# Second attention of a two-layer trunk: reciprocal per head, place of the short rows' parts, banks of the logits, and order of the projections

## The chip, the cores and the metric

The kernel runs on one core of a Trainium2 chip. The metric is the device time of one execution in microseconds (us); the kernel before took 1237.31 us in the median of three runs (1236.33 to 1238.17).

The engines are called as the profile calls them: PE is TensorE (matmuls; PEld its weight loads), DVE is VectorE, ACT is ScalarE, POOL is GpSimd, SP is the queue that issues DMAs. Each engine works through its own instructions in the order of the program and waits where an operand is not there or a buffer is not free.

## The reference, cut to what matters

512 positions of width 1024 go through two layers and a final norm. Layer 0 is a mixer of block-sparse and windowed attention and an MLP; layer 1 is the "forgetting" attention that the change touches, and a second MLP. Cut to that attention:

```python
def fox_mixer(h, w_in, b_forget, w_out):          # 16 heads of 64, Q = 128
    q, k, v, fz = _split(h @ w_in, ODD_SPLITS)
    ...
    log_f = jax.nn.log_sigmoid((fz + b_forget).astype(jnp.float32))
    cum = jnp.cumsum(log_f, axis=1).transpose(0, 2, 1)
    def block(c):                                 # one block of 128 query rows
        ...
        s = (jnp.einsum('bhqd,bhkd->bhqk', qc, k).astype(jnp.float32) * scale
             + cq[..., None] - cum[:, :, None, :])
        p = masked_softmax(s, key_pos[None, :] <= t[:, None])
        return jnp.einsum('bhqk,bhkd->bhqd', p, v).astype(jnp.float32)
    o = lax.map(block, jnp.arange(S // Q))
    ...
    return o.astype(h.dtype) @ w_out
```

## The kernel before, in words

All matmuls that need float32 accuracy are made of parts: an operand is split into a rounded high part and a low part (the rest), and three products are added up in one bank (`mm3`, L129 to L131). `split` makes the parts of a weight: ACT copies the high part (L91), then DVE or POOL subtracts it from the raw weight (L94); the letters of `FOX_LOW` say, tile by tile in the order of use, which of the two.

The stages follow each other: first mixer (0 to about 310 us of the span), first MLP, second attention (`fox`, about 640 to 893 us), second MLP. A scheduler orders every engine's instructions when the program is built; it starts from the order in which the code is written, which in `fox` is the string `FOX_ORDER`: `v0` to `v3` project values of four heads each, `f` makes the forget gates, `k0` to `k7` project queries and keys of a pair of heads (24 matmuls of 512 columns each for q and for k), `p0` to `p7` do the softmax of a pair, and `o01` and the like multiply the outputs of two pairs with the output weights and add them to the residual rows (8 groups of 6 matmuls, each followed by an addition on DVE, L530).

For one head `softmax_t` works on four blocks of query rows, `qi` 3 to 0. Block `qi` sees 128*(qi+1) keys, so a row has 512, 384, 256 or 128 logits; "long rows" are those of qi 3 and 2, "short rows" those of qi 1 and 0. In turn:

- PE makes the logits of a block in two passes into a PSUM bank (L457). The banks come from the tag `s`, which has two; the third block's logits need the bank of the first.
- DVE adds the mask and finds the minimum (L461, written to the tile P), ACT takes the exponential and its sum (L462).
- After two blocks DVE takes their reciprocal (L464) and scales it (L465). This is done twice in a head.
- The long rows' high parts (f16, tile HL) are made by ACT (L473), the short rows' by POOL (L475). The low parts of all rows are made by DVE in one operation with two SBUF inputs (L476).
- When the whole of HL is written, SP issues a transposing DMA to HT (L478).

`turned` widens HT to the parts PTh (ACT, L488) and PTl (POOL, L406); `pv` multiplies them with the values (L499, L500); `combine` (L509, L510) and `split_o` (L406, L515) bring the result into the form that the output projection needs. The list `todo` holds `turned` and `pv` of a head back until the softmax of the next head is written down: the transposition of one head is under way while the next head's logits are worked on. PTh and PTl of a head are ordered behind the instructions that `p_act` and `p_pool` name: the newest exponential of the next head, and its last high part on POOL.

The tiles P, HL, HT, PTh and PTl have two buffers each, and each of the PSUM tags `acc` (projections), `s` (logits), `pt` and `o` has two banks. A projection's bank is freed by its copies and subtractions: for q by ACT L1269 and DVE L402, for k by ACT L1272 and DVE L400, for values by ACT L1220 and DVE L400.

Of the kernel before, what the change touches and what calls it, by code (L numbers as in the profile page):

```python
# [7 lines left out]
F32 = mybir.dt.float32  # L8
# [3 lines left out]
AF = mybir.ActivationFunctionType  # L12
ALU = mybir.AluOpType
AX = mybir.AxisListType

P = 128
S = 512
D = 1024
NT = S // P
# [7 lines left out]
SEG = [0, 128, 384, 768]  # L27
P_UP = 32768.0
PTW = 1280
BANKS = [(0, [(0, 0)]), (512, [(1, 0), (3, 384)]), (1024, [(2, 0)])]  # L30
PTOFF = {0: 0, 1: 512, 3: 896, 2: 1024}
# [11 lines left out]

MIX0_ORDER = "c0 k1 q1 n0 v1 v0 k0 n1 m1 c1 m0 k2 n2 o45 o0 n3 k3 m2 m3 o17 o6 o23"

FOX_ORDER = "v0 f k0 k1 k2 k3 p0 v1 k4 p1 p2 o01 k5 v3 v2 p3 k6 p4 p5 p6 k7 o23 o45 p7 o67"


class Trunk:
# [395 lines left out]
    def softmax_t(self, passes, band):  # L445


        nc = self.nc
        pt = self.pP.tile([P, PTW], F32, tag="P", name=self.nm("P"))
        st = self.sm.tile([P, 3, 4], F32, tag="sst", name=self.nm("sst"))  # L450
        hl = self.pHL.tile([P, 2, PTW], F16, tag="HL", name=self.nm("HL"))
        for q0 in (2, 0):
            for qi in (q0 + 1, q0):
                w = P * (qi + 1)
                ps = self.psum("s")
                for i, (q, k) in enumerate(passes):
                    nc.tensor.matmul(ps[:, :w], q[:, qi * P:(qi + 1) * P], k[:, :w],  # L457
                                     start=i == 0, stop=i == len(passes) - 1)
                seg = pt[:, SEG[qi]:SEG[qi] + w]
                mn, sm = (st[:, a, qi:qi + 1] for a in range(2))  # L460
                nc.vector.tensor_tensor_reduce(seg, ps[:, :w], band[:, S - w:S], 1.0, 3e38, ALU.add, ALU.min, mn)  # L461
                self.p_act = nc.scalar.activation(seg, seg, AF.Exp, bias=mn, scale=-1.0, accum_out=sm)  # L462
            r = st[:, 2, q0:q0 + 2]
            nc.vector.reciprocal(r, st[:, 1, q0:q0 + 2])  # L464
            nc.vector.tensor_scalar(r, r, P_UP, None, op0=ALU.mult)  # L465
            for qi in (q0 + 1, q0):
                r = st[:, 2, qi:qi + 1]
                parts = [(0, min(qi + 1, 3), qi * P)] + ([(3, 4, PTOFF[3])] if qi == 3 else [])
                for j0, j1, off in parts:
                    seg = pt[:, SEG[qi] + j0 * P:SEG[qi] + j1 * P].rearrange("p (j c) -> p j c", c=P)  # L470
                    view = lambda a: hl[:, a, off:].rearrange("p (j c) -> p j c", c=P)[:, 0:3 * (j1 - j0 - 1) + 1:3, :]
                    if q0 == 2:
                        nc.scalar.activation(view(0), seg, AF.Copy, scale=r)  # L473
                    else:
                        self.p_pool = nc.gpsimd.tensor_scalar(view(0), seg, r, 1.0, op0=ALU.mult, op1=ALU.mult)  # L475
                    nc.vector.scalar_tensor_tensor(view(1), seg, r, view(0), op0=ALU.mult, op1=ALU.subtract)  # L476
        t = self.pHT.tile([P, 2 * PTW // P, P], F16, tag="HT", name=self.nm("HT"))
        nc.sync.dma_start_transpose(t, hl.rearrange("p a b -> p (a b)"))  # L478
        return t

    def turned(self, t):


        tv = t.rearrange("p (a b) c -> p a (b c)", a=2)
        hi = self.pPT.tile([P, PTW], FR, tag="PTh", name=self.nm("PTh"))
        lo = self.pPT.tile([P, PTW], FR, tag="PTl", name=self.nm("PTl"))
        with self.tc.issue_after(self.p_act.ins):
            self.nc.scalar.activation(hi, tv[:, 0], AF.Copy)  # L488
        with self.tc.issue_after(self.p_pool.ins):
            self.round(lo, tv[:, 1])  # L490
        return hi, lo

# [689 lines left out]
    def fox(self, hs):  # L1182
        self.phase, self.pieces = FOX_LOW, 0
        nc, I = self.nc, self.I
        w = I["odd_w_in"][0]
        wo = I["odd_w_out"][0]
        lo, hi = slice(0, HD), slice(HD, P)
        with ExitStack() as cx:
# [4 lines left out]
            self.pHT = pool("fHT", 2)  # L1193
            o2 = pool("fo", 2)
            a1 = cx.enter_context(self.tc.tile_pool(name="attf1", bufs=1))
            wv = self.cols(w, [(2048, 2304), (3072, 3088)])
            x = self.norm_t(hs, self.row_tile(I["mix_norm"][1], "g"))
            zt = a1.tile([P, NT, 16], F32, name="zt")
            band = a1.tile([P, S], F32, name="mband")
# [101 lines left out]
            st, o = {}, {}  # L1301

            def step(op, arg):
                if op == "v":
                    values(int(arg))
                elif op == "f":
                    forget()
                elif op == "k":
                    st[int(arg)] = qk(int(arg))
                elif op == "p":  # L1310
                    pair(int(arg), st[int(arg)])
                elif op == "o":
                    pairs = [int(a) for a in arg]
                    if pairs[-1] not in o:
                        behind()
                    self.out_proj(wo, pairs, [o[a] for a in pairs], hs)

            for s in FOX_ORDER.split():
                step(s[0], s[1:])
# [41 lines left out]
```

## Time and profile before

| | |
|---|---|
| median of three runs | 1237.31 us (1236.33 to 1238.17) |
| the profiled execution | 1239.53 us |
| its span, first to last instruction | 1237.8 us |
| mean granted TensorE clock | 0.991 |
| second attention, 640 to 900 us: PE busy | 240.26 of 260 us |
| DVE, ACT and POOL busy there | 193.38, 159.35 and 111.87 us |

All durations are of the one profiled execution. Busy times count an instruction from its start to its end; matmuls follow each other before the one ahead has ended, so the mean of one matmul (383 ns for 512 columns) is longer than the step from one to the next. "PE acc L129 <- DVE Q L402: 2.6, 3, 1.6" reads: PE, at line 129 with a bank `acc`, stood idle 2.6 us in all and three times, 1.6 us at the longest, until DVE had finished line 402. The granted clock (PEclk) is the share of full speed that PE was given in a stretch.

### The profile page before, as it was taken

The numbers are of one execution on the slowest core, as the hardware profiler recorded it, in microseconds if no ns is written. First come the engines' busy times: TensorE is split into PE (matmuls) and PEld (weight loads), VectorE is DVE, ScalarE is ACT, GpSimd is POOL, SyncE is SP. The second block draws the span as 40 slices with busy tenths as digits, with TensorE's granted clock in tenths as the row PEclk, the third lists the DMA queues.
The fourth block names the chain that finished last, engine by engine and source line by source line (L and its number), as shares of the span: only waits on it lengthen the run. The fifth ranks groups of instructions, "written<-read, shape, count | busy, mean of one in ns | idle before, by whom it ended". The sixth has DMA issues, their size and how long they took to land.

```text
span 1237.8 us, 16953 instructions
## 1 busy us (share of the span) xinstructions
PE 1201.4 (97%) x6055; PEld 1011.2 (82%) x6055; DVE 986.7 (80%) x1683; ACT 672.7 (54%) x1211; POOL 481.3 (39%) x470
## 2 busy tenths in 40 slices
PE   9999999999999999999999889998899999999997
PEld 7879987887888888888887777887798888888886
DVE  6877678788878897789775778749787898789875
ACT  6447666675654455445436666647455444544542
POOL 3434457553543233323003453535345323332214
PEclk9999999999999999999999989999999999999999
DMA  7961232131533324333024544644563333332301
GB/s 231 336 179 53 86 102 78 51 112 52 153 102 102 102 87 119 106 99 95 26 69 130 117 100 112 135 123 89 150 169 104 96 92 120 102 103 88 98 1 69
DMA packets 183440, 134.25 MB, mean 108 GB/s; under 512 B 47875, under 2 KB 158635, under 8 KB 183356
## 3 DMA queue, kind: packets, MB, share of 16 engines
q1 hardware_dynamic: 183196, 132.94, 38.3%
q8 instruction: 48, 0.79, 0.3%
q14 instruction: 36, 0.29, 0.1%
q10 hardware_dynamic: 160, 0.23, 0.1%
HBM read 120.27 MB, written 7.64 MB: 103 GB/s over the span
## 4 chain that ended last, share of the span: by engine, by line
PE 61%; DVE 8%; ACT 2%; DMA 2%; issue 2%; POOL 1%; DVEq 0%; ACTq 0%; POOLq 0%
PE s L1123 12%; PE acc L131 11%; PE acc L129 11%; PE acc L130 11%; PE o L1123 6%; PE pt L1123 3%; DVE HL L476 2%; DMA HT<-HL 2%; DVE P L461 1%; DVE whl L94 1%; PE s L131 1%; PE s L130 1%; PE s L129 1%; PE s L457 1%; DVE x L530 1%
## 5 line engine op out<-in xcount | busy, mean ns | idle before, releaser
L129 PE MATMUL acc<-xhi,whl 128*128 128x512 f32 (+1 forms) x768 | 293.9, 383 | 2.8 <-DVE Q L402 2.5
L131 PE MATMUL acc<-xhi,whl 128*128 128x512 f32 (+1 forms) x768 | 294.3, 383 | 1.4 <-POOL whl L94 0.8
L130 PE MATMUL acc<-xlo,whl 128*128 128x512 f32 (+1 forms) x768 | 292.9, 381 | 0.0
L94 DVE TENSOR_TENSOR whl<-raw,whl 128x1024 fp32r<-128x1024 f32 (+2 forms) x110 | 161.7, 1473 | 84.8 <-ACT whl L91 68.5
L1026 POOL TENSOR_TENSOR r<-r,yrow 128x512 f32<-128x512 f32 x64 | 98.3, 1536 | 317.4 <-ACT r L1025 317.4
L91 ACT ACTIVATE whl<-raw 128x1024 fp32r<-128x1024 f32 (+1 forms) x139 | 145.0, 1048 | 47.5 <-PE acc L131 27.9
L131 PEld LDWEIGHTS acc<-xhi,whl 128*128 128x128 f32 x768 | 144.5, 188 | 30.4 <-DVE whl L94 1.6
L129 PEld LDWEIGHTS acc<-xhi,whl 128*128 128x128 f32 x768 | 144.4, 188 | 30.5 <-issue 2.4
L1123 PE MATMUL s<-whl,sp 128*128 128x512 f32 x672 | 167.6, 390 | 0.0
L130 PEld LDWEIGHTS acc<-xlo,whl 128*128 128x128 f32 x768 | 144.7, 188 | 26.4
L1123 PEld LDWEIGHTS s<-whl,sp 128*128 128x128 f32 x672 | 126.2, 188 | 26.6
L1077 ACT ACTIVATE whl<-w 128x1024 fp32r<-128x1024 f32 x98 | 103.6, 1059 | 71.2 <-PE s L1123 43.5
L1078 DVE TENSOR_TENSOR whl<-w,whl 128x1024 fp32r<-128x1024 f32 x98 | 134.9, 1378 | 8.5 <-ACT whl L1077 8.5
L1025 ACT ACTIVATE r<-acc 128x512 f32<-128x512 f32 x62 | 37.1, 598 | 117.0 <-PE acc L131 117.0
L94 POOL TENSOR_TENSOR whl<-raw,whl 128x1024 fp32r<-128x1024 f32 x29 | 71.1, 2454 | 51.2 <-ACT whl L91 49.7
L1123 PE MATMUL o<-whl,sp 128*128 128x512 f32 x336 | 88.8, 391 | 0.0
L1083 DVE TENSOR_TENSOR w<-w,w 128x1024 f32<-128x1024 f32 x56 | 82.0, 1464 | 1.0
L1131 DVE TENSOR_TENSOR x<-s,x 128x512 f32<-128x512 f32 x112 | 74.8, 679 | 3.0 <-PE s L1123 3.0
L1123 PEld LDWEIGHTS o<-whl,sp 128*128 128x128 f32 x336 | 63.3, 188 | 13.6
L400 DVE TENSOR_TENSOR sp<-act,sp 128x512 fp32r<-128x512 f32 x64 | 69.5, 1107 | 0.6 <-ACT sp L1034 0.6
L1028 ACT ACTIVATE act<-r 128x512 f32<-128x512 f32 x64 | 40.5, 633 | 45.8 <-POOL r L1026 45.7
L422 ACT ACTIVATE P<-P,sst 128x128 f32<-128x128 f32 (+1 forms) x96 | 53.3, 557 | 14.4 <-DVE sst L421 12.6
(291 smaller groups left out, 2493.9 us busy)
## 6 DMA issues: line engine op xcount, KB each, us to landing
raw<-in_mlp_w SPq DMA_DIRECT2D x72, 512.0 KB
w<-in_mlp_w SPq DMA_DIRECT2D x56, 512.0 KB
raw<-in_odd_w_in SPq DMA_DIRECT2D x22, 512.0 KB
raw<-in_even_w_in SPq DMA_DIRECT2D x20, 512.0 KB
band<-bias_dram SPq DMA_DIRECT2D x24, 256.0 KB
bias_dram<-bias_rows SPq DMA_DIRECT2D x16, 320.0 KB
raw<-in_even_w_out SPq DMA_DIRECT2D x8, 512.0 KB
raw<-in_odd_w_out SPq DMA_DIRECT2D x8, 512.0 KB
```

The costliest lines, as they stand in the source:

```text
L91: nc.scalar.activation(hl[:, 0, :n], raw[:, :n], AF.Copy)
L94: eng.tensor_tensor(hl[:, 1, :n], raw[:, :n], hl[:, 0, :n].bitcast(F32), op=ALU.subtract)
L129: mm(ps, ahl[0], bhl[0], start=first, stop=False)
L130: mm(ps, ahl[0], bhl[1], start=False, stop=False)
L131: mm(ps, ahl[1], bhl[0], start=False, stop=last)
L400: self.nc.vector.tensor_tensor(out, ps, hi.bitcast(F32), op=ALU.subtract)
L1026: nc.gpsimd.tensor_tensor(r, r, row, op=ALU.mult)
L1077: nc.scalar.activation(t[:, 0], src, AF.Copy)
L1078: nc.vector.tensor_tensor(t[:, 1], src, t[:, 0].bitcast(F32), op=ALU.subtract)
L1083: nc.vector.tensor_tensor(out, a_, b_, op=op)
L1123: mm = lambda l, r, first, last: nc.tensor.matmul(ps, l, r, start=first, stop=last, skip_group_check=True)
L1131: nc.vector.tensor_tensor(hv, ps, hv, op=ALU.add)
```

## The change

It has five parts, all of them in the second attention.

1. The reciprocal and its scaling are done once in a head, behind all four exponentials (new L462, L463), on four elements a row instead of twice on two. The scaling multiplies by a small tile `p_up`, filled once, and no longer by a number.
2. Short rows: POOL multiplies P by the reciprocal in place (new L467, two instructions), ACT copies the high parts (new L471, 256 and 128 columns), and POOL subtracts them for the low parts (new L472). Long rows stay with ACT and DVE (new L478, L479). In a head this takes two operations of DVE away, adds two to ACT, and makes two of POOL four.
3. The logits use the banks of `s` and `pt` in turn, so that a head has four.
4. PTh is ordered behind the last high part of the next head and no longer behind its last exponential; PTl behind its last low part on POOL.
5. `FOX_ORDER`: key, query and value projections stand between the pairs of heads one at a time, and `o45` stands behind the last pair.

```diff
-FOX_ORDER = "v0 f k0 k1 k2 k3 p0 v1 k4 p1 p2 o01 k5 v3 v2 p3 k6 p4 p5 p6 k7 o23 o45 p7 o67"
+FOX_ORDER = "v0 f k0 k1 p0 k2 v1 p1 k3 p2 o01 k4 v2 p3 k5 p4 k6 v3 p5 k7 p6 o23 p7 o45 o67"
...
-        for q0 in (2, 0):
-            for qi in (q0 + 1, q0):
-                w = P * (qi + 1)
-                ps = self.psum("s")
...
-            r = st[:, 2, q0:q0 + 2]
-            nc.vector.reciprocal(r, st[:, 1, q0:q0 + 2])
-            nc.vector.tensor_scalar(r, r, P_UP, None, op0=ALU.mult)
-            for qi in (q0 + 1, q0):
...
-                    if q0 == 2:
-                        nc.scalar.activation(view(0), seg, AF.Copy, scale=r)
-                    else:
-                        self.p_pool = nc.gpsimd.tensor_scalar(view(0), seg, r, 1.0, op0=ALU.mult, op1=ALU.mult)
-                    nc.vector.scalar_tensor_tensor(view(1), seg, r, view(0), op0=ALU.mult, op1=ALU.subtract)
+        for qi in (3, 2, 1, 0):
+            w = P * (qi + 1)
+            ps = self.psum("s" if qi % 2 else "pt")
...
+        nc.vector.reciprocal(st[:, 2], st[:, 1])
+        nc.vector.tensor_tensor(st[:, 2], st[:, 2], self.p_up, op=ALU.mult)
+        blocks = lambda v, off, n, step: v[:, off:].rearrange("p (j c) -> p j c", c=P)[:, 0:step * (n - 1) + 1:step, :]
+        for qi in (1, 0):
+            seg = pt[:, SEG[qi]:SEG[qi] + P * (qi + 1)]
+            nc.gpsimd.tensor_scalar(seg, seg, st[:, 2, qi:qi + 1], 1.0, op0=ALU.mult, op1=ALU.mult)
+        for a, off, n in ((0, 0, 2), (2 * P, PTOFF[1], 1)):
+            seg = pt[:, a:a + n * P]
+            h, l = (hl[:, i, off:off + n * P] for i in range(2))
+            self.p_act = nc.scalar.activation(h, seg, AF.Copy)
+            self.p_low = nc.gpsimd.tensor_tensor(l, seg, h, op=ALU.subtract)
+        for qi in (3, 2):
+            r = st[:, 2, qi:qi + 1]
+            for j0, n, off in ((0, 3, qi * P), (3, 1, PTOFF[3]))[:qi - 1]:
+                seg = blocks(pt, SEG[qi] + j0 * P, n, 1)
+                h, l = (blocks(hl[:, i], off, n, 3) for i in range(2))
+                self.p_act = nc.scalar.activation(h, seg, AF.Copy, scale=r)
+                nc.vector.scalar_tensor_tensor(l, seg, r, h, op0=ALU.mult, op1=ALU.subtract)
...
-        with self.tc.issue_after(self.p_pool.ins):
+        with self.tc.issue_after(self.p_low.ins):
             self.round(lo, tv[:, 1])
...
+            self.p_up = a1.tile([P, NT], F32, name="pup")
+            nc.gpsimd.memset(self.p_up, P_UP)
```

What the scheduler makes of it is seen in the order of the built programs. In the rows below a row is a line of the code, an operation, what it writes and reads, and the size; names carry buffer numbers. Line numbers of the change are those of its own text.

On PE, at the first head of the second attention (s and pt are logits' banks, acc a projection's), before:

```order
L131 MATMUL acc_6543<-xhi_6182,whl_6540 128x512
L457 MATMUL s_6794<-K_971_6516,Q_969_6514 128x512
L457 MATMUL s_6799<-K_971_6516,Q_969_6514 128x384
L457 MATMUL s_6794<-K_972_6517,Q_970_6515 128x512
L457 MATMUL s_6799<-K_972_6517,Q_970_6515 128x384
L129 MATMUL acc_6573<-xhi_6182,whl_6570 128x512
L130 MATMUL acc_6573<-xlo_6183,whl_6570 128x512
```

and with the change:

```order
L131 MATMUL acc_6545<-xhi_6184,whl_6542 128x512
L456 MATMUL s_6628<-K_971_6518,Q_969_6516 128x512
L456 MATMUL pt_6633<-K_971_6518,Q_969_6516 128x384
L456 MATMUL s_6628<-K_972_6519,Q_970_6517 128x512
L456 MATMUL pt_6633<-K_972_6519,Q_970_6517 128x384
L456 MATMUL s_6638<-K_971_6518,Q_969_6516 128x256
L456 MATMUL s_6638<-K_972_6519,Q_970_6517 128x256
L456 MATMUL pt_6643<-K_971_6518,Q_969_6516 128x128
L456 MATMUL pt_6643<-K_972_6519,Q_970_6517 128x128
L129 MATMUL acc_6575<-xhi_6184,whl_6572 128x512
```

The head starts at the same place; its four blocks now stand together, while before the logits of 256 and 128 columns stood 22 matmuls further on.

On ACT, at the second head (P, HL and sst with the middle numbers are its tiles, PTh is the first head's), before:

```order
L462 ACTIVATE P_6830,sst_6831<-P_6830,sst_6831 128x128
L473 ACTIVATE HL_6832<-P_6830,sst_6831 128x3x128
L473 ACTIVATE HL_6832<-P_6830,sst_6831 128x128
L473 ACTIVATE HL_6832<-P_6830,sst_6831 128x3x128
L462 ACTIVATE P_7087,sst_7088<-P_7087,sst_7088 128x512
L488 ACTIVATE PTh_6869<-HT_6828 128x1280
L462 ACTIVATE P_7087,sst_7088<-P_7087,sst_7088 128x384
```

and with the change:

```order
L461 ACTIVATE P_6664,sst_6665<-P_6664,sst_6665 128x128
L1277 ACTIVATE K_989_6614<-acc_6575 64x512
L478 ACTIVATE HL_6666<-P_6664,sst_6665 128x3x128
L478 ACTIVATE HL_6666<-P_6664,sst_6665 128x128
L478 ACTIVATE HL_6666<-P_6664,sst_6665 128x3x128
L491 ACTIVATE PTh_6703<-HT_6662 128x1280
L471 ACTIVATE HL_6666<-P_6664 128x128
L471 ACTIVATE HL_6666<-P_6664 128x256
L1274 ACTIVATE Q_1017_6778<-acc_6723 64x512
```

The second head's two short copies now stand behind the first head's PTh, which waits for a transposition; a copy that frees a projection's bank (L1274) stands behind them.

On POOL, at the first two heads, before:

```order
L475 TENSOR_SCALAR HL_6793<-P_6791,sst_6792 128x2x128
L475 TENSOR_SCALAR HL_6793<-P_6791,sst_6792 128x128
L475 TENSOR_SCALAR HL_6832<-P_6830,sst_6831 128x2x128
L475 TENSOR_SCALAR HL_6832<-P_6830,sst_6831 128x128
L406 TENSOR_SCALAR PTl_6870<-HT_6828 128x1280
```

and with the change:

```order
L467 TENSOR_SCALAR P_6625<-P_6625,sst_6626 128x256
L467 TENSOR_SCALAR P_6625<-P_6625,sst_6626 128x128
L472 TENSOR_TENSOR HL_6627<-P_6625,HL_6627 128x128
L472 TENSOR_TENSOR HL_6627<-P_6625,HL_6627 128x256
L406 TENSOR_SCALAR K_985_6602<-K_985_6602 64x512
L94 TENSOR_TENSOR whl_6806<-raw_6802,whl_6806 128x1024
L467 TENSOR_SCALAR P_6664<-P_6664,sst_6665 128x256
L467 TENSOR_SCALAR P_6664<-P_6664,sst_6665 128x128
L406 TENSOR_SCALAR K_989_6614<-K_989_6614 64x512
L472 TENSOR_TENSOR HL_6666<-P_6664,HL_6666 128x128
L406 TENSOR_SCALAR PTl_6704<-HT_6662 128x1280
L472 TENSOR_TENSOR HL_6666<-P_6664,HL_6666 128x256
```

Two instructions of a head became four, and the second head's last subtraction stands behind the first head's PTl.

More of the change, by code (lines that the diff above doesn't have):

```diff
@@ L451, in softmax_t @@
         hl = self.pHL.tile([P, 2, PTW], F16, tag="HL", name=self.nm("HL"))
-        for q0 in (2, 0):
-            for qi in (q0 + 1, q0):
-                w = P * (qi + 1)
-                ps = self.psum("s")
[L456 to L462, printed above, removed]
-            r = st[:, 2, q0:q0 + 2]
-            nc.vector.reciprocal(r, st[:, 1, q0:q0 + 2])
-            nc.vector.tensor_scalar(r, r, P_UP, None, op0=ALU.mult)
-            for qi in (q0 + 1, q0):
[L467 to L471, printed above, removed]
-                    if q0 == 2:
-                        nc.scalar.activation(view(0), seg, AF.Copy, scale=r)
-                    else:
-                        self.p_pool = nc.gpsimd.tensor_scalar(view(0), seg, r, 1.0, op0=ALU.mult, op1=ALU.mult)
-                    nc.vector.scalar_tensor_tensor(view(1), seg, r, view(0), op0=ALU.mult, op1=ALU.subtract)
@@ new lines, in softmax_t @@
+        for qi in (3, 2, 1, 0):
+            w = P * (qi + 1)
+            ps = self.psum("s" if qi % 2 else "pt")
+            for i, (q, k) in enumerate(passes):
+                nc.tensor.matmul(ps[:, :w], q[:, qi * P:(qi + 1) * P], k[:, :w],
+                                 start=i == 0, stop=i == len(passes) - 1)
+            seg = pt[:, SEG[qi]:SEG[qi] + w]
+            mn, sm = (st[:, a, qi:qi + 1] for a in range(2))
+            nc.vector.tensor_tensor_reduce(seg, ps[:, :w], band[:, S - w:S], 1.0, 3e38, ALU.add, ALU.min, mn)
+            self.p_act = nc.scalar.activation(seg, seg, AF.Exp, bias=mn, scale=-1.0, accum_out=sm)
```

## The prediction

> **What bounds the kernel now.** I read the page's first two parts, then the windows of the second attention (cut by pairs of heads), then who PE waited for there.
>
> ```profile
> PE 1201.4 (97%) x6055; PEld 1011.2 (82%) x6055; DVE 986.7 (80%) x1683; ACT 672.7 (54%) x1211; POOL 481.3 (39%) x470
> ...
> PEclk9999999999999999999999989999999999999999
> ```
>
> PE is the bound of the whole, but slices 22, 23, 27 and 28 of its row (not shown) hold an 8, and one slice has a lower clock: all in the second attention. The windows say how much; their columns are length, busy time of each engine (instructions), granted clock, DMA share, GB/s.
>
> ```profile
> 672.00:745.00 73.00, 64.63 (x327) 54.15 (x326) 54.57 (x141) 52.12 (x112) 34.34 (x37) 0.93 0.49 111
> 745.00:790.00 45.00, 41.92 (x199) 34.58 (x198) 38.33 (x77) 27.33 (x54) 25.13 (x26) 0.96 0.56 127
> 790.00:832.00 42.00, 42.00 (x280) 38.94 (x280) 22.29 (x53) 22.21 (x45) 15.96 (x16) 1.00 0.48 113
> 832.00:893.00 61.00, 54.03 (x248) 42.86 (x247) 51.21 (x108) 36.21 (x75) 28.34 (x26) 0.97 0.53 129
> sum 221.00, PE 202.58 PEld 170.52 DVE 166.40 ACT 137.88 POOL 103.78; mean PE 50.65 PEld 42.63 DVE 41.60 ACT 34.47 POOL 25.94
> ```
>
> Of 221 us PE stands idle 18.4: 8.4, 3.1, 0 and 7.0 by stretch. Besides, the clock: 7% of 73, 4% of 45 and 3% of 61 us are 5.1 + 1.8 + 1.8 = 8.7 us lost. **At most 27.1 us can be had**, and no engine beside PE is near full: DVE with 166 of 221 is the next. So it is waits in a chain, not load. The same stretch's waits of PE:
>
> ```profile
> PE s L457 <- DVE sst L461: 5.1, 5, 1.7
> PE acc L129 <- DVE x L530: 4.3, 3, 2.7
> PE o L499 <- ACT PTh L488: 3.1, 3, 1.9
> PE acc L129 <- DVE Q L402: 2.6, 3, 1.6
> PE s L457 <- POOL K L406: 1.8, 2, 1.5
> PE o L500 <- POOL PTl L406: 0.8, 1, 0.8
> PE acc L131 <- POOL O L515: 0.4, 1, 0.4
> ```
>
> Logits waiting for a bank lead, then projections waiting for DVE, and only then the transposed softmax (3.9 us).
>
> **The change, part by part.**
>
> ```profile
> L476 DVE SCALAR_TENSOR_TENSOR HL<-P,sst,HL 128x128 f16<-128x128 f32 x32 | 19.0, 596 | 0.0
> L476 DVE SCALAR_TENSOR_TENSOR HL<-P,sst,HL 128x256 f16<-128x256 f32 x16 | 11.0, 687 | 3.6 <-POOL HL L475 3.5
> L464 DVE RECIPROCAL sst<-sst 128x2 f32<-128x2 f32 x32 | 5.0, 157 | 8.3 <-ACT P L462 8.1
> L465 DVE TENSOR_SCALAR sst<-sst 128x2 f32<-128x2 f32 x32 | 13.5, 423 | 0.6
> L475 POOL TENSOR_SCALAR HL<-P,sst 128x256 f16<-128x256 f32 x16 | 9.0, 560 | 44.9 <-DVE sst L465 39.4 <-DVE sst L464 2.7 <-ACT PTh L488 1.7
> L424 POOL TENSOR_SCALAR P<-P,sst 128x256 f32<-128x256 f32 x8 | 4.6, 580 | 5.9 <-DVE sst L423 5.7 <-POOL KS L406 0.2
> L1140 POOL TENSOR_TENSOR xn<-x,gf 128x256 f32<-128x256 f32 x2 | 1.5, 732 | 0.0
> L473 ACT ACTIVATE HL<-P,sst 128x384 f16<-128x384 f32 x32 | 19.4, 605 | 13.3 <-DVE sst L465 13.0 <-DVE sst L464 0.3
> L473 ACT ACTIVATE HL<-P,sst 128x128 f16<-128x128 f32 x16 | 6.2, 388 | 0.0
> L461 DVE CUSTOM_DVE_ANT_0 P<-s,mband 128x512 f32<-128x512 f32 x16 | 11.0, 685 | 7.0 <-PE s L457 6.6
> ```
>
> *Load.* In each of 16 heads DVE loses 0.687 + 0.596 (short lows), 0.157 and 0.423: 1.86 us, 30 us in all. ACT gains copies of 128 and 256 columns: 0.39 and, between 0.39 and 0.61, say 0.50; 14 us in all. POOL's scaling costs what it did (0.580 for 0.560); two subtractions come on top, 0.73 for 256 columns (the row has f32 out, not f16) and for 128 between 0.39, as one input costs on ACT, and 0.73; I take 0.45, the 256 row being mostly per column; 19 us in all. After it DVE has 137, ACT 152, POOL 123 of some 210 us: none becomes full. The scaling by `p_up`, four elements, I take as its predecessor's usual 0.17; ends 0.15 and 2.26, see the row below. Filling `p_up` is one POOL instruction before any head: nothing.
>
> *Chain of a head.* With four banks the four blocks follow each other on PE (2560 columns), on DVE and on ACT. The long rows' reciprocal now waits for the short rows' exponentials, about 1 us later; the short rows' parts run on POOL beside the long rows' on ACT and DVE. The chain to the transposition stays about as long; the row of logits waiting for L461 (5.1 us) loses its cause, unless heads follow each other faster than DVE's four minima (0.69 for the longest, some 2.2 us with their sums' reading), which the order has once (heads 12 and 13). I leave 0.8.
>
> *First five heads (672 to 745).* Here the projections stand close and ACT decides when a bank is free. PE's speed and ACT's packed times:
>
> ```profile
> 655.00:665.00 10.00, 9.98 (x44) 8.29 (x45) 7.63 (x10) 5.90 (x9) 1.23 (x3) 1.00 0.67 168
> 800.00:810.00 10.00, 10.00 (x83) 9.82 (x82) 7.16 (x21) 5.88 (x16) 1.23 (x2) 1.00 0.92 186
> ...
> 671.75 0.56 PE L457 MATMUL s<-K,Q 128*128 128x512 f32 x2
> ...
> 674.81 0.73 ACT L462 ACTIVATE P<-P,sst 128x512 f32<-128x512 f32 x1
> 675.53 0.60 ACT L462 ACTIVATE P<-P,sst 128x384 f32<-128x384 f32 x1
> ...
> 676.72 1.41 ACT L473 ACTIVATE HL<-P,sst 128x384 f16<-128x384 f32 x3 [0.49 <-DVE sst L465]
> ...
> L488 ACT ACTIVATE PTh<-HT 128x1280 fp32r<-128x1280 f16 x16 | 20.3, 1266 | 11.1 <-DMA HT<-HL 11.1
> L1269 ACT ACTIVATE Q<-acc 64x512 fp32r<-64x512 f32 x16 | 9.5, 591 | 11.9 <-PE acc L131 9.6 <-DVE Q L402 1.7 <-PE s L457 0.4
> L91 ACT ACTIVATE whl<-raw 128x1024 fp32r<-128x1024 f32 x33 | 34.3, 1049 | 3.5 <-PE acc L131 3.4
> ```
>
> PE steps 10/44 = 0.227 us for 512 columns, 0.120 in a value projection. From the first logits to the second value block of `v1` the new order has 72 projection matmuls (16.3), 24 of values (2.9), logits of five heads and pv of two (seven times 2560 columns, 1.14 each: 8.0): 27.2 us. That block needs the bank of the key projection of `k2`, freed by an ACT copy which has, from the first exponential on, 44 instructions ahead: exponentials of four heads (0.72 + 0.60 + 0.50 + 0.39 + 0.19 for the last sum, 2.4 a head: 9.6), three heads' long highs (1.41 each: 4.2) and short copies (0.9: 2.7), two PTh (2.5), seven copies of q and k with the one itself (4.1), three weights (3.1), one copy each for o and v (1.0): 27.2. The first exponential starts 3.1 us behind the first logits, DVE's subtraction follows (0.7): 31.0. **PE waits about 3.8 us there**; between 0, if the copy gets ahead, and 6, if nothing overlaps. With 0.8 for logits, and 1.7 for the clock (a third of the present 5.1, for one wait in place of nine), this stretch loses 6.3 for 13.5.
>
> *Output projections (745 to 790, 832 to 893).* Each group of six matmuls (1.4 us) needs the addition of the second-last group, and DVE does it in between.
>
> ```profile
> 863.59 3.17 POOL L94 TENSOR_TENSOR whl<-raw,whl 128x1024 fp32r<-128x1024 f32 x1 [1.21 <-ACT whl L91]
> ...
> 864.63 2.15 DVE L465 TENSOR_SCALAR sst<-sst 128x2 f32<-128x2 f32 x1
> 866.70 1.09 DVE L476 SCALAR_TENSOR_TENSOR HL<-P,sst,HL 128x384 f16<-128x384 f32 x2
> 867.71 0.68 DVE L530 TENSOR_TENSOR x<-acc,x 128x512 f32<-128x512 f32 x1
> ...
> 868.45 0.79 PE L129 MATMUL acc<-whl,O 128*128 128x512 f32 x1 [2.68 <-DVE x L530]
> L465 DVE TENSOR_SCALAR sst<-sst x32: 151/170/2257, 676.5 to 864.6; 128x2 f32<-128x2 f32 x32
> ```
>
> The longest wait came from two elements: L465 took 2.15 us until POOL's weight was done, and the addition stood behind it. The change has half as many of these scalings. It puts a pair's heads beside `o01` and beside `o23`; behind two additions stand four minima (2.2 us) and a reciprocal, so I count 2 us of waits at each place. The first stretch then loses 2.0 for 4.9; the last 2.0, 1.0 for a pv behind its PTh, 1.0 of O and x at the end (as now: 0.4 and one x), 0.7 of clock: 4.7 for 8.8. Between them, now without loss, I add 1.0 since heads 10 to 13 stand there.
>
> *pv.* `o45` behind the last pair and one projection between pairs put 17 to 35 us of PE work, at the speeds above, from a head's last logits to its pv (10 to 39 before, eight heads under 14.5). A DMA takes 5.2 us and PTh 1.3:
>
> ```profile
> 686.75 5.17 DMA HT<-HL
> ```
>
> so the 3.9 us of pv waits go, but for the 1.0 above. SP's queue: weights ahead of a transposition wait for one of five raw buffers, freed a projection earlier; cost nothing, 5 us if one were late.
>
> *Sum.* 6.3 + 2.0 + 1.0 + 4.7 = 14.0 left of 27.1 to 27.2: 13 us less. The profiled execution took 1239.5 us (span 1237.8 and 1.7 around it), 2.2 above the median of 1237.3; so 1226.5 for such an execution, **1224 us** for the median.
>
> **Two rules beside it.** The clock fell with no idle time of PE over 2.7 us in the row above. The Trainium skill ("TensorE: Matmul & The Clock Gate", Part 1) has the clock halve after an idle window of about 3.4 us; by it none of the present waits costs clock, the trace disagrees, and the gain, without the clock's part, would be 7 us. The skill's "GPSIMD Engine Reference" (Engine selection) has two-input work about twice as slow on GpSimd as on VectorE, which speaks against part 2. The rows have 0.732 on POOL against 0.687 on DVE for 256 columns; by the rule the two subtractions would take 2.6 us a head and lengthen the chain by 1.4, still under the 17 us of cover.
>
> **The rivals.** (a) *DVE and POOL block each other.* For: the 2.15 us above. POOL gets 19 us more, and DVE's long lows still have two SBUF inputs. Against: DVE has 30 us less to do. If half of the gain goes into it: 1231. (b) *Slower: the chain through ACT.* A head's short copies stand behind the PTh of the head ahead, which waits for its transposition. One turn is then 5.2 + 1.3 + 0.4 (copy) + 0.4 (subtraction) + 1.4 (PTl) + 0.7 = 9.4 us, while PE needs 27.2/4.5, some 6, per head; heads 0 to 5 and 10 to 13 would lose 3.4 each, eight times 27, and the clock its 8.7 again: 1237.3 - 27.1 + 35.9, about 1246. It decides from the point where the lag exceeds the cover, some 3 us at head 0; the order has the tight sequence at three heads only (1, 3, 11). (c) *Everything goes:* 1237.3 - 25 (all but 2 us at the end) = 1212. (d) *The waits only move* from L461 to ACT's copies, first five heads losing 12 instead of 6, and the clock stays: no more than 1 us is gained, 1236.5.
>
> **How the numbers follow.** Forecast 0.55, own range 1216 to 1230; (a) 0.17; (b) 0.10; (c) 0.06; (d) 0.12. Some 0.2% (2.5 us) is what a measurement of this kernel can tell from none. Faster: forecast, (a), (c) and a little of (d), 0.80; same, the most of (d), 0.10; slower (b), 0.10. The range 1215 to 1237 leaves out (b), most of (c) and little else.
>
> **What would show it.** In the profile of the changed kernel: the wait of logits for L460 under 1 us; one wait of `acc` of some 4 us around 27 us behind the first logits, ended by ACT or DVE with a copy of K; DVE busy 30 us less; granted clock over 0.97 from 672 to 745; PE idle 9 to 13 us from the first logits to the last output projection. It would be wrong if pv waits for PTh or PTl more than 3 us in all, or if the new scaling L463 has durations of 2 us at more than five heads.

## The result, and the profile after

| | before | after |
|---|---|---|
| median of four runs each | 1237.53 us (1236.33 to 1238.17) | 1219.30 us (1217.06 to 1223.81) |
| ratio to before, 95% interval | | 0.9858 (0.9828 to 0.9889) |
| the profiled execution, span | 1239.53, 1237.8 us | 1223.81, 1222.1 us |

The change takes off 18.2 us; 13 were forecast. The profiled execution of after is the longest of its four, 4.5 us above their median. From 60 to 80 us, in the first mixer, where the change does nothing, its granted clock is 0.83, which costs 3.4 us. Its mean clock is 0.991, that of the other three 0.995 and 0.996, so most of the 4.5 us is lost clock that they did not have.

The page of after, busy times and PE's clock in 40 slices:

```profile
PE 1196.8 (98%) x6055; PEld 1011.4 (83%) x6055; DVE 966.5 (79%) x1619; ACT 679.3 (56%) x1243; POOL 501.9 (41%) x503
...
PEclk9989999999999999999999989999999999999999
```

The third slice is that spell of low clock. The dip that the clock had in the second attention before is still there: one 8, in the same slice. The windows of after, cut at the same times as before (columns as before):

```profile
672.00:745.00 73.00, 70.13 (x371) 61.21 (x370) 55.10 (x128) 56.07 (x132) 46.25 (x53) 0.95 0.55 129
745.00:790.00 45.00, 45.00 (x258) 39.59 (x257) 26.92 (x55) 29.99 (x61) 28.40 (x31) 1.00 0.63 141
790.00:832.00 42.00, 40.22 (x233) 36.30 (x232) 29.20 (x70) 34.35 (x77) 25.45 (x30) 0.96 0.48 103
832.00:893.00 61.00, 60.28 (x331) 50.76 (x330) 47.90 (x94) 33.73 (x68) 27.73 (x29) 1.00 0.60 157
sum 221.00, PE 215.63 PEld 187.85 DVE 159.12 ACT 154.14 POOL 127.84; mean PE 53.91 PEld 46.96 DVE 39.78 ACT 38.54 POOL 31.96
```

By stretch PE now stands idle 2.9, 0, 1.8 and 0.7 us, 5.4 in all; before it was 18.4. The clock takes 5% of 73 and 4% of 42 us, 5.3, for 8.7 before. All of PE's waits of those stretches stand in four rows (us in total, times, longest):

```profile
PE acc L129 <- DVE K L400: 1.8, 1, 1.8
PE acc L129 <- DVE v L400: 1.5, 1, 1.5
PE s L456 <- POOL K L406: 1.3, 1, 1.3
PE acc L129 <- DVE x L533: 0.6, 2, 0.3
```

No logits wait for a bank any more, and no pv waits for its PTh or PTl. Of the waits for x 0.6 us remain. The new and changed operations, grouped by line and shape (count, busy time, mean ns, idle before):

```profile
L479 DVE SCALAR_TENSOR_TENSOR HL<-P,sst,HL 128x384 f16<-128x384 f32 x32 | 28.1, 877 | 4.4 <-ACT HL L478 4.2
L472 POOL TENSOR_TENSOR HL<-P,HL 128x256 f16<-128x256 f32 x16 | 13.7, 856 | 1.1 <-ACT HL L471 1.1
L472 POOL TENSOR_TENSOR HL<-P,HL 128x128 f16<-128x128 f32 x16 | 9.0, 566 | 8.1 <-ACT HL L471 8.0
L479 DVE SCALAR_TENSOR_TENSOR HL<-P,sst,HL 128x128 f16<-128x128 f32 x16 | 8.3, 522 | 0.0
L471 ACT ACTIVATE HL<-P 128x256 f16<-128x256 f32 x16 | 6.4, 403 | 0.0
L463 DVE TENSOR_TENSOR sst<-sst,pup 128x4 f32<-128x4 f32 x16 | 6.0, 374 | 0.4
L471 ACT ACTIVATE HL<-P 128x128 f16<-128x128 f32 x16 | 4.7, 295 | 0.0
L462 DVE RECIPROCAL sst<-sst 128x4 f32<-128x4 f32 x16 | 2.8, 176 | 10.7 <-ACT P L461 10.7
```

And the timeline of after around the wait for v (start, duration, engine, line, operation; in brackets the idle time ahead and what ended it):

```profile
704.25 2.36 POOL L94 TENSOR_TENSOR whl<-raw,whl 128x1024 fp32r<-128x1024 f32 x1 [0.31 <-ACT whl L91]
...
704.53 0.18 DVE L462 RECIPROCAL sst<-sst 128x4 f32<-128x4 f32 x1 [0.65 <-ACT P L461]
...
704.75 1.89 DVE L463 TENSOR_TENSOR sst<-sst,pup 128x4 f32<-128x4 f32 x1
...
706.56 0.41 DVE L400 TENSOR_TENSOR v<-acc,v 128x256 fp32r<-128x256 f32 x1
...
707.02 0.58 PE L129 MATMUL acc<-whl,xhi 128*128 128x256 f32 x1 [1.53 <-DVE v L400]
```

Four elements took 1.89 us, beside POOL's subtraction for a weight that started 0.5 us earlier and ended at 706.61. The subtraction of v, which frees PE's bank, stood behind it. The one-input reciprocal, inside the same subtraction of POOL, took its usual 0.18.

### The profile page after: what moved, and what is told of

It reads as the page before. It is cut to its first block, busy times and chain, and to the rows that moved or that the text cites. A ratio compares the mean times of both kernels' runs of the same rounds, so it can differ in the third digit from the quotient of the medians.

```text
span 1222.1 us, 16954 instructions
## 1 busy us (share of the span) xinstructions
PE 1196.8 (98%) x6055; PEld 1011.4 (83%) x6055; DVE 966.5 (79%) x1619; ACT 679.3 (56%) x1243; POOL 501.9 (41%) x503
## 4 chain that ended last, share of the span: by engine, by line
PE 68%; DVE 3%; ACT 2%; issue 1%; DMA 1%; POOL 0%; DVEq 0%; ACTq 0%; POOLq 0%
PE acc L129 13%; PE acc L131 13%; PE acc L130 13%; PE s L1126 13%; PE o L1126 6%; PE pt L1126 3%; PE s L130 1%; PE s L131 1%; PE s L129 1%; PE o L503 1%; PE o L502 1%; PE s L456 1%; PE o L131 1%; PE o L130 1%; PE o L129 1%
## 5 line engine op out<-in xcount | busy, mean ns | idle before, releaser
L94 DVE TENSOR_TENSOR whl<-raw,whl 128x1024 fp32r<-128x1024 f32 (+2 forms) x110 | 164.2, 1497 | 82.2 <-ACT whl L91 73.6
L422 ACT ACTIVATE P<-P,sst 128x128 f32<-128x128 f32 (+1 forms) x96 | 53.3, 557 | 14.4 <-DVE sst L421 12.6
```

The source lines that it names most:

```text
L94: eng.tensor_tensor(hl[:, 1, :n], raw[:, :n], hl[:, 0, :n].bitcast(F32), op=ALU.subtract)
```

## The experiments

Every kernel below was timed beside the kernel before, which took 1237.3 to 1238.0 us in each group. PE's idle time is 228 us less its busy time in the windows from 672 to 900 us; the clock's loss is the sum of (1 - granted clock) times length over 672 to 745, 745 to 790, 790 to 832 and 832 to 900 us, both of the profiled execution, which is not the median one. The granted clock has two digits, so the second is good to about 1 us. "Steps" are the reciprocal steps per head; "moved" says whether the short rows' parts are made as in the change. The kernels with one step also have the change's fourth part (PTh and PTl ordered behind later instructions) and write the short rows' parts ahead of the long rows': no run separates these from the single reciprocal.

| kernel | order, steps, banks, moved | median us (lowest to highest) | ratio to before (95%) | PE idle, clock lost |
|---|---|---|---|---|
| before | old, 2, 2, no | 1237.5 | 1 | 18.4, 8.9 |
| order alone | new, 2, 2, no | 1224.9 (1224.2 to 1225.5) | 0.9891 (0.9872 to 0.9911) | 11.3, 3.7 |
| banks alone | old, 2, 4, no | 1231.3 (1229.1 to 1233.9) | 0.9948 (0.9932 to 0.9965) | 16.1, 3.5 |
| order and banks | new, 2, 4, no | 1230.8 (1226.2 to 1234.7) | 0.9942 (0.9922 to 0.9962) | 13.3, 5.2 |
| order and one step | new, 1, 2, no | 1231.7 (1230.3 to 1238.5) | 0.9954 (0.9939 to 0.9970) | 13.5, 5.3 |
| change with two banks | new, 1, 2, yes | 1232.3 (1230.6 to 1233.6) | 0.9951 (0.9933 to 0.9969) | 14.2, 6.6 |
| change, short parts as before | new, 1, 4, no | 1222.1 (1221.6 to 1226.9) | 0.9877 (0.9857 to 0.9898) | 8.1, 3.1 |
| change, old order | old, 1, 4, yes | 1224.6 (1222.9 to 1225.6) | 0.9888 (0.9868 to 0.9907) | 10.8, 1.5 |
| after | new, 1, 4, yes | 1219.3 (1217.1 to 1223.8) | 0.9858 (0.9828 to 0.9889) | 5.4, 5.3 |

I took the time of each profiled execution, less its idle time and lost clock (and less the first mixer's spell, where it has one). All nine come to between 1209.7 and 1213.9 us: these two account for the differences between the profiled executions within some 2 us.

**Order alone.** The kernel before with one line changed:

```diff
-FOX_ORDER = "v0 f k0 k1 k2 k3 p0 v1 k4 p1 p2 o01 k5 v3 v2 p3 k6 p4 p5 p6 k7 o23 o45 p7 o67"
+FOX_ORDER = "v0 f k0 k1 p0 k2 v1 p1 k3 p2 o01 k4 v2 p3 k5 p4 k6 v3 p5 k7 p6 o23 p7 o45 o67"
```

> The kernel before with the new order of the second attention and nothing else. Theory A (each wait of TensorE in the profile before has its own cause, so the parts add): the waits for PTh and PTl (3.9 us) and about half of those for x, Q and K go, with their share of the clock, while the logits' 5.1 us for a bank stay: about 9 us less than before, 1228 us. Theory B (the order only pays with four banks and the shorter vector work, since heads that stand closer to projections wait for the same engines): not more than 3 us less, 1234 to 1238 us, with the logits' wait for L461 above 8 us.

Measured 12.6 us less, more than either theory gave. PE's waits in this kernel:

```profile
PE acc L129 <- DVE Q L402: 4.7, 5, 1.6
PE s L457 <- DVE sst L461: 2.3, 3, 1.2
PE acc L129 <- DVE K L400: 2.1, 2, 1.9
PE o L499 <- ACT PTh L488: 1.4, 1, 1.4
PE acc L129 <- DVE x L530: 0.8, 3, 0.3
```

The order took away more than half of the logits' waits for a bank too (2.3 for 5.1), which had been put down to the banks, and nearly all of the waits for x. The waits for Q grew, from 2.6 to 4.7 us; theory A had half of them go.

**The change with the old order.** The same line, turned back in the kernel after.

> The changed kernel with the old order of the second attention. Theory A (parts add): the waits for PTh and PTl return and the projections crowd the first heads, logits no longer wait: 9 us more than the changed kernel, about 1228 us. Theory B (the order only pays with the other parts and they with it): the kernel falls back to 1234 to 1238 us.

Measured 5.3 us above after, less than either theory gave. All the parts but the order gain 13.0 us, the order alone 12.6, all together 18.2: they share some 7 us. A wait that either can remove counts once for each of them when they are run alone, and once in all when they are run together.

**The change with two banks.** All logits take the tag `s`:

```diff
-            ps = self.psum("s" if qi % 2 else "pt")
+            ps = self.psum("s")
```

> The changed kernel with all logits in the two banks of tag s. Theory A (the wait of logits for L461, 5.1 us before, came from the banks): 4 to 6 us and some clock more than the changed kernel, about 1225 us, and the wait for L460 appears in the waits of TensorE with over 4 us. Rival C (that wait came from the reciprocal and its scaling between the two halves on VectorE, which are gone; with one reciprocal per head two banks do): within 1 us of the changed kernel and the wait for L460 under 1 us.

Measured 13 us above after, over twice what theory A gave. Its waits:

```profile
PE o L503 <- POOL PTl L406: 3.0, 2, 1.6
PE s L456 <- DVE sst L460: 2.8, 3, 1.8
PE acc L129 <- DVE x L533: 2.2, 4, 0.6
PE acc L129 <- POOL O L406: 2.0, 1, 2.0
```

Only 2.8 us are logits waiting for a bank, where theory A had over 4; the rest is late work on POOL and DVE. C is out. That this kernel is also slower than the order alone, with the same two banks, was expected by neither.

**The change with the short rows' parts as before**, highs by POOL, lows by DVE, one reciprocal step and four banks kept:

```diff
-            self.p_act = nc.scalar.activation(h, seg, AF.Copy)
-            self.p_low = nc.gpsimd.tensor_tensor(l, seg, h, op=ALU.subtract)
+            self.p_low = nc.gpsimd.tensor_scalar(h, seg, r, 1.0, op0=ALU.mult, op1=ALU.mult)
+            nc.vector.scalar_tensor_tensor(l, seg, r, h, op0=ALU.mult, op1=ALU.subtract)
```

> The changed kernel with the short rows' high parts on GpSimd and low parts on VectorE as before (rounded high from the scaled product, low by a fused multiply and subtract), one reciprocal step and four banks kept. Theory A (VectorE is not near full, only its order counts): VectorE busy about 20 us more, 1 to 3 us slower by additions to x and subtractions for K that come later, about 1221 us. Rival D (the relief of VectorE is the main gain): 6 us or more slower, 1226 us or above, with waits of TensorE for VectorE of over 8 us. Rival E (moving the short parts only exchanged engines): within 1 us of the changed kernel.

Measured 2.8 us above after, the size that theory A gave. The two ranges and the two intervals overlap, so that the short parts gain anything, against E, is likely and not settled. D's 6 us or more did not come. DVE is busy only 8 us more (974.6 for 966.5), not 20. The part meant to relieve DVE is the smallest.

**Banks alone**, in the kernel before, the tags as in the change:

```diff
-                ps = self.psum("s")
+                ps = self.psum("s" if qi % 2 else "pt")
```

> The kernel before with the logits in four banks (tags s and pt in turn) and nothing else: two reciprocal steps per head, the old order. Theory F (the 5.1 us that logits waited for L461 came from the banks): this wait goes with its share of the clock, 5 to 8 us less than before, 1230 to 1232 us. Rival G (the second half's logits stand behind the first half's reciprocal and scaling on VectorE, whatever the banks, and the other waits take over): not more than 2 us less, 1235 to 1238 us.

Measured 6.0 us less: theory F in time. No logits wait for L461 in it, but the idle time falls by 2.3 us only and the clock's loss by 5.4, so F's wait went, but other waits took the place of more than half of it.

**Order and banks**, both edits in the kernel before.

> The kernel before with the new order and four banks; two reciprocal steps per head and the short rows' parts as before. Against the run with the new order alone (1224.9 us) it shows the banks, against the run with one reciprocal and the short rows' parts as before (1222.1 us) the single reciprocal step. Theory A (parts add): the 2.3 us of logits' waits left with the new order go, 1222 to 1223 us, and the single reciprocal is worth under 1 us. Rival G (the reciprocal steps count): 1224 to 1225.5 us, the wait for VectorE moved from logits to the projections' banks.

Neither: 1230.8 us, 5.9 above the order alone. Put on top of the new order, four banks lose time as long as there are two reciprocal steps. The longest wait of this kernel, in its timeline:

```profile
822.14 1.05 POOL L475 TENSOR_SCALAR HL<-P,sst 128x256 f16<-128x256 f32 x2 [1.11 <-DVE sst L465]
...
822.88 1.64 DVE L476 SCALAR_TENSOR_TENSOR HL<-P,sst,HL 128x256 f16<-128x256 f32 x4 [0.38 <-POOL HL L475]
824.45 0.41 DVE L400 TENSOR_TENSOR v<-acc,v 128x256 fp32r<-128x256 f32 x1
...
824.91 0.50 PE L129 MATMUL acc<-xhi,whl 128*128 128x512 f32 x1 [2.42 <-DVE v L400]
```

DVE stands idle 0.38 us for POOL's short highs, makes four low parts in 1.64 us, and only then frees PE's bank.

**Scaling on ACT.** In the kernel after:

```diff
-        nc.vector.tensor_tensor(st[:, 2], st[:, 2], self.p_up, op=ALU.mult)
+        nc.scalar.activation(st[:, 2], st[:, 2], AF.Copy, scale=P_UP)
```

> The changed kernel with the scaling of the reciprocals (L463, four elements, 1.89 us once at the second value block of v1 beside GpSimd's subtraction for a weight) done by ScalarE. Theory H (that held instruction makes the 1.5 us wait of a projection for v and the half-clock spell behind it): the wait for v L400 is under 0.4 us and the time 1.5 to 4 us under the changed kernel's, 1215 to 1218 us. Rival I (ScalarE's own queue sets that place and 16 more instructions of 0.2 us lengthen it): within 1 us of the changed kernel's 1219.3 or above, with waits for Q, K or v that ScalarE's copies end.

1219.4 us (1219.2 to 1220.9), ratio 0.9852 (0.9838 to 0.9867): no change. The wait for v halves to 0.7 us, and the clock of the profiled execution is whole in all stretches. But logits wait 2.9 us once for K, whose rounding stands on POOL behind a PTl that waits for its transposition, and a pv waits 2.0 us for PTh. Idle time is 9.7 us, lost clock 0. This is rival I in time, though not by ACT's queue. Theory H is borne out in part: the wait at the place it named got shorter, but not below its 0.4 us.

**All weights' lows on DVE** (`FOX_LOW = "D"`).

> The changed kernel with all weights' low parts of the second attention on VectorE (14 that GpSimd did in 2.4 us each go to VectorE at 1.2 us each, 17 us more there). Theory H (GpSimd's long subtractions hold VectorE's small instructions): L463 takes over 1 us nowhere, L479's mean falls from 0.88 to below 0.75 us, and the time is 1 to 3 us less, 1216 to 1218 us. Rival J (VectorE's load weighs more than the holding): 1 to 4 us slower, 1220 to 1223 us, by waits for K, v, Q and x behind the weights' lows.

1225.0 us (1223.2 to 1226.1), ratio 0.9892 (0.9874 to 0.9910): rival J, and by more than its 1 to 4 us. By the trace it is 13 weights, not 14. L463 takes 0.55 us at most, as H had it, but the long lows still 0.79 us, and the time rises by 5.7: taken as a whole, POOL's share of the weights pays.

**Values first.** One line of the kernel after:

```diff
-FOX_ORDER = "v0 f k0 k1 p0 k2 v1 p1 k3 p2 o01 k4 v2 p3 k5 p4 k6 v3 p5 k7 p6 o23 p7 o45 o67"
+FOX_ORDER = "v0 f k0 k1 p0 v1 k2 p1 k3 p2 o01 v2 k4 p3 k5 p4 v3 k6 p5 k7 p6 o23 p7 o45 o67"
```

> The changed kernel with the value projections v1, v2 and v3 each put ahead of the query and key projection beside them (p0 v1 k2 ..., o01 v2 k4 ..., p4 v3 k6 ...). Theory K (the two waits left of a second value block, 1.5 us at v1 and 1.8 us at v3 with 5.1 us lost by the clock behind them, arise because a value block of 2.9 us follows a key projection whose bank the second block needs; a value block's bank is freed by one short copy and one short subtraction): both waits go and the clock stays above 0.98 in all four stretches, 1212 to 1216 us. Rival L (the waits move to the logits behind the later K, or to the projection of Q behind the values): within 1.5 us of the changed kernel's 1219.3 or above.

1228.9 us (1226.4 to 1234.5), ratio 0.9928 (0.9908 to 0.9949): theory K falls. The wait at v3 is gone, but a value block of v1 waits 2.6 us at its new place, for the subtraction of K. That stands on DVE behind a reciprocal that waits for exponentials, its scaling and a minimum. Additions to x are late seven times, 4.2 us in all. So the wait goes with the head's vector work beside a projection, and did not need a value block behind a key projection in the old place.

**Order and one step**: the kernel with the short parts as before, and two banks.

> The changed kernel with two banks for the logits and the short rows' parts on GpSimd and VectorE as before: only the new order and the single reciprocal step are left of the change. Runs so far: new order alone 1224.9 us, new order with four banks 1230.8, with one step and four banks 1222.1, with one step, moved parts and two banks 1232.3. Theory M (one reciprocal step and four banks need each other: with two banks the long rows' parts wait for the short rows' logits, which wait for a bank): 1229 to 1234 us, some 5 us or more above the new order alone. Rival N (with two banks it was the moved short parts that lost, by PTl behind GpSimd's subtractions): 1223 to 1226 us.

1231.7 us (1230.3 to 1238.5): theory M. With the new order, going from two banks to four costs 5.9 us with two reciprocal steps and gains 9.5 with one; going from two steps to one (with what hangs on it, as said above) costs 6.7 with two banks and gains 8.7 with four. In this kernel logits wait for banks again (three times):

```profile
PE s L456 <- DVE sst L460: 3.7, 3, 2.1
PE acc L129 <- DVE Q L402: 3.5, 4, 1.9
PE acc L129 <- DVE x L531: 3.2, 5, 2.3
```

**Two weights' lows on DVE**, those beside the waits for v and K, found by their times in the trace:

```diff
-FOX_LOW = "DDDPDDDPPPDPDPDDDDPPDPDDDPDPDPDPDD"
+FOX_LOW = "DDDPDDDPPPDDDPDDDDPPDPDDDDDPDPDPDD"
```

> The changed kernel with the two weights' low parts that GpSimd makes at the second value blocks of v1 and v3 (2.4 us each, at 704 and 807 us) made by VectorE instead (1.2 us each); the other twelve stay on GpSimd. Theory H (GpSimd's long subtraction holds the scaling of the reciprocals there, and the subtractions for K and v stand behind it): no L463 over 1 us at these two places, the waits of projections for K and v in all under 2 us instead of 3.3, 1216 to 1218 us. Rival J (VectorE then does 1.2 us of its own at the same place, ahead of the same subtractions): waits of 2 to 3.5 us as now, within 1 us of the changed kernel's 1219.3.

1220.6 us (1219.7 to 1224.6), ratio 0.9861 (0.9842 to 0.9880). The place is H's: no L463 above 0.86 us, the waits of projections for K and v fall from 3.3 to 0.3 us, and from 672 to 832 us the clock is whole. The time is nearer to J's, 1.3 us above after. In the profiled execution the last stretch got worse, by the same thing in larger form:

```profile
844.44 2.46 POOL L94 TENSOR_TENSOR whl<-raw,whl 128x1024 fp32r<-128x1024 f32 x1 [0.18 <-ACT whl L91]
...
844.60 3.38 DVE L94 TENSOR_TENSOR whl<-raw,whl 128x1024 fp32r<-128x1024 f32 x1
846.86 2.05 POOL L472 TENSOR_TENSOR HL<-P,HL 128x128 f16<-128x128 f32 x2
...
848.04 0.50 PE L130 MATMUL acc<-whl,O 128*128 128x512 f32 x1 [2.27 <-DVE whl L94]
```

POOL started 0.16 us earlier; DVE's 1.2 us became 3.38. PE lost 2.3 us here, 2.0 for O later, and the clock 8% of 68 us. This execution is the longest of its five, 3.9 us above their median; its mean clock is 0.994, that of the others 0.996 and 0.997, so they lost less of the clock.

**Three weights' lows on DVE**: that one too.

```diff
-FOX_LOW = "DDDPDDDPPPDDDPDDDDPPDPDDDDDPDPDPDD"
+FOX_LOW = "DDDPDDDPPPDDDPDDDDPPDPDDDDDPDPDDDD"
```

> The run before with one more weight's low part moved from GpSimd to VectorE: that of the last weight of o67, which in the run before ran from 844.4 us beside VectorE's own subtraction for a weight (3.38 us there, 1.2 alone) and had a subtraction for the last head and the rounding of O behind it. Theory H (GpSimd's and VectorE's long subtractions hold each other, and what stands behind them is late): the waits of 2.3 us for whl and 2.0 us for O in the last stretch fall below 1 us in all, the waits at v1 and v3 stay small, the clock of the last stretch is above 0.98: 1214 to 1218 us, under the changed kernel's 1219.3. Rival P (waits of this size turn up elsewhere whenever the instructions shift, whatever is taken away): idle time of TensorE from 672 to 900 us as in the run before or more, 1219 to 1223 us.

1216.2 us (1215.8 to 1218.4), ratio 0.9820 (0.9792 to 0.9848): theory H. The windows of this kernel:

```profile
672.00:745.00 73.00, 70.56 (x381) 60.55 (x380) 60.18 (x139) 62.05 (x142) 46.16 (x57) 1.00 0.52 119
745.00:790.00 45.00, 45.00 (x262) 39.98 (x261) 24.54 (x49) 27.57 (x53) 25.56 (x27) 1.00 0.66 150
790.00:832.00 42.00, 41.17 (x240) 35.86 (x239) 34.59 (x73) 33.77 (x76) 28.11 (x32) 1.00 0.59 127
832.00:893.00 61.00, 58.96 (x343) 50.31 (x342) 50.12 (x93) 35.82 (x71) 21.52 (x24) 1.00 0.49 134
```

The waits for whl and O of the last stretch fall to 0.6 us, as H had it; an addition to x is late once instead, by 1.6 us. The clock is whole in all four rows; PE is idle 5.3 us, as in after. So what the profiled execution gains on that of after is the clock's, not idle time. This kernel has the lowest median of all. Its interval still overlaps that of after, so that it beats after is likely, not settled.

## Why the prediction was right, point by point

**Right in kind, short in size.** The time lies in the forecast's own range: the waits went, and no rival took their place as a whole. Against the terms of what was to be left over:

| term | forecast to be left, us | left, us |
|---|---|---|
| first five heads, 672 to 745: logits | 0.8 | 0 |
| the same: a projection's bank | 3.8 | 1.5, and 1.3 for a rounding of K |
| the same: clock | 1.7 | 3.6 |
| place of `o01`, 745 to 790 | 2.0 | 0 |
| heads 10 to 13 | 1.0 | 1.8, and 1.7 of clock |
| last stretch | 4.7 | 0.7 |
| sum | 14.0 | 10.7 |

**The mis-sized terms are the output projections.** For `o01` and `o23` the prediction put four minima and a reciprocal between two additions, 2 us of waits at each; measured are 0 and 0.6. One pv behind its PTh (1.0) and 0.7 of clock at the end did not come either. That is 6.0 us too much; against it heads 10 to 13 were put 2.5 us too small, and the first five heads 0.2. In the first five heads this is luck: 3.1 us too much for logits and the bank, made up by a rounding of K that was not foreseen (1.3) and by 1.9 too little for the clock. With 10.7 us left of 27.1 the gain would be 16.4; the other 1.8 us to the measured 18.2 lie outside these terms and stay open. The order alone already takes the waits for x from 4.3 to 0.8 us, so DVE's lighter load was not needed for that.

What the prediction left out is in the timeline of after at `o01`:

```profile
738.37 0.69 DVE L460 CUSTOM_DVE_ANT_0 P<-s,mband 128x512 f32<-128x512 f32 x1
...
740.00 0.63 PE L456 MATMUL s<-K,Q 128*128 128x512 f32 x2
...
740.02 1.28 DVE L533 TENSOR_TENSOR x<-acc,x 128x512 f32<-128x512 f32 x2
...
741.24 0.45 PE L129 MATMUL acc<-whl,O 128*128 128x512 f32 x1
```

DVE does work through four minima (738.37 to 740.02) ahead of two additions. But PE, which needs the first of them for its next group, has the logits of the next head in between (740.00 to 741.24). By then the first addition is done, and the second ends at 741.30. A head brings 1.2 us of PE's work along with the minima that it puts on DVE.

**The bank at v1: place right, cause wrong in part.** The wait came 30 us behind the first logits (705.5 against 675.6) where 27 to 31 were worked out, and a subtraction on DVE ended it. But the prediction put 3.8 us there and named the key projection's bank, freed late by ACT's queue. It was 1.5 us and the bank of the first value block: K's second subtraction starts at 707.6, after PE had gone on. ACT's copy of v was done at 704.8; DVE's subtraction of v stood behind L463, held by POOL. With the two weights moved, the wait falls to 0.3 us. The prediction had the price in its row for L465 (2.15 us) and used it only for the loss that would go.

**Load.** The lows in DVE fall from 53.5 us (23.5 for the long groups and the 19.0 and 11.0 shown) to 36.4, scaling from 13.5 to 6.0, reciprocals from 5.0 to 2.8: 27 less, for 30. DVE as a whole is busy only 20 us less (986.7 and 966.5). The long lows got slower; before they were:

```profile
L476 DVE SCALAR_TENSOR_TENSOR HL<-P,sst,HL 128x384 f16<-128x384 f32 x32 | 23.5, 735 | 1.9 <-ACT HL L473 1.9
```

That is 735 ns before and 877 after. The shortest took 0.60 us in both, the longest 2.0 and 2.2: the means hold some that were held up. Two of those in after took 1.56 and 1.41 us and began while an earlier operation of POOL still had 1.2 and 1.0 us to run. It is not the weights alone: with three of them moved off POOL the mean is 944 ns. ACT's copies took 0.40 and 0.30 (0.50 and 0.39 assumed, 11 us in all for 14); POOL's subtractions 0.86 and 0.57 (0.73 and 0.45). By the Trainium skill, "GPSIMD Engine Reference" (Engine selection), two-input work is about twice as slow on GpSimd. Here the shortest subtraction of POOL (after) and the shortest low of DVE (before) are 0.67 and 0.47 us for 256 columns, 0.43 and 0.34 for 128, but 2.4 and 1.2 for the weights' 1024, so in these rows it holds for the long ones only.

**The signs.** Logits waiting for L460 under 1 us: held, none. One wait of `acc` of some 4 us at v1, ended by a copy of K: held for the place, failed for the size (1.5 us) and for the operand (v). DVE busy 30 us less: failed, 20. Clock above 0.97 in the first stretch: failed, 0.95. Idle 9 to 13 us: failed, 5.4. What would have shown it wrong did not come: no pv waits, and L463 took about 2 us once.

**The rivals.** (a), DVE and POOL block each other, did not take half of the gain, but the blocking is real: it makes the wait for v and, when the instructions shift, others. Moving three of POOL's weights away was worth some 3 us, if anything (the intervals overlap). (b) fell: no pv waits in the changed kernel. With two banks the wait for PTl is there (3.0 us), but not at (b)'s price. (c), 1212 us, was too far even for the best run. (d) fell: the first five heads lost 2.9 us of idle time, not 12.

**What the prediction took for granted.** It gave each part waits of its own. The runs show that with the new order one reciprocal step (with the fourth part) and four banks pay only together, and that order and the rest share 7 us. How each alone comes to lose 6 to 7 us with the new order is shown only in its waits (banks, Q and x with one step; v and K with four banks); the chain behind them was not taken apart and stays open.

## What to carry to other kernels

Parts of a change that shorten one chain should be run alone and in pairs. Here, in the new order, two of them cost 6 and 7 us apart and gained 3 together, and a sum of waits by what ended them did not tell of it. When a wait is ended by a short vector instruction, look at what GpSimd runs at that moment, and at what stands behind it in its engine's queue. One changed letter of a placement can move a wait and not remove it: read the whole stretch's idle time and clock before calling it a gain.

## What the hardware did that was not expected

**Either engine holds the other.** In after, DVE's and POOL's subtractions for weights met once more, at 852.7 us:

```profile
852.72 1.21 DVE L94 TENSOR_TENSOR whl<-raw,whl 128x1024 fp32r<-128x1024 f32 x1
852.75 3.44 POOL L94 TENSOR_TENSOR whl<-raw,whl 128x1024 fp32r<-128x1024 f32 x1
```

Here DVE was first by 0.03 us and POOL's took 3.44 us for 2.4; in the run with two weights moved it was the other way round. In the three rows shown the later one is lengthened by about the time that the earlier one still runs: by 2.2 us for 2.3, by 1.0 for 1.2 and, for the four elements of L463, by 1.7 for 1.9. The Trainium skill, "SBUF — State Buffer" (SBUF: two separate sides), has the two engines share a port pair which the first to start locks for its whole instruction, against DVE's operations with two SBUF inputs or in a two-port mode; these rows agree.

**The clock follows the idle time in a fixed window, not the length of a wait.** In every profile but the two that have none, the spells of half clock within the execution last 3.41 us, or two or three times that, and start, in each profile, on one grid of 3.41 us. In after, the wait of 1.3 us and the beginning of the one of 1.5 leave PE idle for 1.46 us in one window of that grid, and half clock follows, for two windows (the first is shown):

```profile
702.26:705.67 3.41, 1.95 (x13) 1.51 (x11) 1.78 (x3) 3.34 (x9) 2.03 (x2) 1.00 0.83 156
705.67:709.08 3.41, 2.06 (x9) 2.06 (x10) 3.35 (x8) 2.69 (x5) 2.39 (x4) 0.50 0.55 129
```

With the scaling on ACT one wait of 2.9 us, at the logits ahead of that place, cost none. It lies across an edge of the grid, and the two windows hold 1.71 and 1.19 us of idle time:

```profile
694.07:697.48 3.41, 1.70 (x15) 1.50 (x13) 2.28 (x5) 3.38 (x9) 1.00 (x2) 1.00 0.95 209
697.48:700.89 3.41, 2.22 (x13) 2.04 (x14) 0.94 (x3) 3.38 (x8) 3.24 (x3) 1.00 0.76 142
```

Over all 14 profiles, 17 windows at full clock held 1.73 us of idle time or more, half a window, and half clock followed all of them. It followed 10 of the 70 with 0.99 to 1.72 us, and none of the 4850 with less; what decides between is open. The rule weighed in the prediction (the Trainium skill, "TensorE: Matmul & The Clock Gate", Part 1: an idle window of about 3.4 us) agrees with the length of the window, but here half a window of idle time was enough. So one wait of 2.9 us went free by where it fell, and shorter waits that fell into one window cost. In the kernel with the scaling on ACT the profiled execution's mean clock is 0.998 and that of the other three 0.996. In after's profiled execution the loss from 672 to 900 us is 5.3 us, as much as all idle time that is left.
